# Attention of a two-layer DiT on one core: the last heads' group with its context blocks first and output-projection pieces between its steps, and the queries' rotary product moved from POOL to VectorE

## The chip, the core and the metric

The kernel runs on one core of a Trainium2 chip. A core has TensorE (matrix products; PE in the profile, its weight loads PEld), VectorE (DVE), ScalarE (ACT), GpSimd (POOL) and SyncE (SP, which here issues most of the transfers). Each engine runs its own instructions in a fixed order, written by a planner at build time from the program's dependences and order, and waits at the head of its queue. SBUF is the working memory, PSUM holds matrix products in banks of 512 columns of fp32. The metric is the device time of one execution in microseconds; comparisons go by medians of several runs.

## The reference

The model is two layers over 512 latent tokens and 256 context tokens, width 1024. Layer 0 is windowed attention (16 heads of 64, four key heads, so four heads' groups), layer 1 is retention; each layer modulates by adaLN and has a SwiGLU FFN. What the change touches is in layer 0:

```python
q_x = rope_2d(rms_norm(q_x.reshape(B, S, N_HEADS, HEAD_DIM), q_gain), tables)
...
def block(b):
    ...
    p = jax.nn.softmax(jnp.concatenate([s_ctx, s_loc, sink_col], axis=-1), axis=-1)
    return (jnp.einsum('bkgqn,bnkd->bqkgd', p[..., :L], v_c)
            + jnp.einsum('bkgqn,bnkd->bqkgd', p[..., L:L + band], vb))
o_x = jnp.moveaxis(lax.map(block, jnp.arange(nb)), 0, 1).reshape(B, S, qd)
out_x = o_x @ w_o
...
p_c = jax.nn.softmax(jnp.concatenate([s_c, sink_col], axis=-1), axis=-1)
out_c = jnp.einsum('bkgqn,bnkd->bqkgd', p_c[..., :L], v_c).reshape(B, L, qd) @ w_o
...
x = x + mx[2] * out_x
x = x + mx[5] * swiglu(modulate(rms_norm(x, norm2_g[i]), mx[3], mx[4]), ffn_w_in[i], ffn_w_out[i])
```

Latent queries of a 128-token block attend to their window and to all context keys; context queries to the context alone. The context stream runs through the same output projection and FFN.

## The kernel before

Tokens lie on the free axis and features on the partitions, in eight chunks of 128 (KT = 8). Large products are made of three fp32r matmuls (`mm3`, lines 148 to 150): each operand is split into a high and a low part, and hi·hi, lo·hi and hi·lo are added in PSUM. A weight tile of 128x1024 is loaded by SP (`w_raw`, line 122, two buffers), cast by ScalarE into its high part (line 140) and subtracted by VectorE into its low part (line 141); `w_parts` says in which pool the two halves lie (two buffers each in `rp`, which lives to the end, and some in the pool of the stage).

Attention runs in four heads' groups, g = 0 to 3. In each group come four latent blocks of 128 queries, (0, 0) to (0, 3), and two context blocks, (1, 0) and (1, 1). A block (`attend`) has three steps. `score` (line 684) makes the scores of four heads on TensorE; VectorE adds the mask and takes the minimum (685), ScalarE exponentiates and sums (line 101), VectorE takes the reciprocal (695) and POOL scales the probabilities (698). `turns` (704) transposes them on TensorE, two pairs of heads at a time, and ScalarE or VectorE copies the result out of PSUM (708). `output` (731) multiplies by the values. In groups 0 to 2 the result is kept raw and split later (`split_o`); in group 3 it is split straight into the operand of the output projection (line 741). `o_t[s][k]` is that operand, s being the stream (0 latent, 1 context) and k the chunk: group g makes k = 2g and 2g + 1.

`make_q` makes the queries of two heads at a time: 48 matmuls into two `pj` banks, the norm's sums (line 590), and for the latent stream the rotary embedding: a shuffle of the partitions (569, VectorE), a product with the cosines (570, POOL), one with the sines (571, VectorE), and the sum (572, VectorE), before the queries are split (578 to 581). Groups 0 to 2 hold two such calls each, behind blocks (0, 1) and (0, 3).

Behind the groups the residual streams are loaded (lines 809 and 810) and the attention's pools closed. The output projection follows in lines 821 to 835: weights in two sets of four, for each set the latent chunks d and then the context chunks. A chunk is 24 matmuls of 512 or 256 columns into a `pj` bank (two banks in all), a gated add into the residual (`gated_add`, 253), and a square added to the sum for the next norm (`add_square`, 207 to 210). Behind some chunks stand adaLN tiles (`ada_tile`): SP loads a 512 KB tile (268, three buffers), and VectorE reduces it against the condition row, once for each stream (271). Eight tiles give the last columns of shift and scale (parts 3 and 4) of the FFN. The condition row (`cond_rows`, 258) is loaded and passed through SiLU first. After the last chunks `fold_gain` (114), `rms` (217 and 194 to 198) and `latent_shape` (877 to 879) shape the FFN's operand, and the FFN's first products (X and Y) begin.

The planner may place an instruction ahead of its written place on its engine when it finds it ready; the written order is its priority. The memory of a closed pool is taken by later pools, tile by tile, when the earlier tile's last reader is done.

Of the kernel before, what the change touches and what calls it, by code (L numbers as in the profile page):

```python
# [14 lines left out]
P = 128  # L15
D = 1024
KT = D // P
# [8 lines left out]
RH = 4  # L26
EPS = 1e-6
UNITS = (4, 5, 8, 6)
WO_ADA = [(0, d) for d in range(7)] + [(1, 2)]
SPLIT_AT = (2, 4)  # L30
HALVES = (slice(0, 256), slice(256, 512))

# [17 lines left out]
def dit_kernel(ctx, tc, xT, cT, crow, small, consts, masks, tabs0, tabs1, jtab, adaQ, adaN, adaT, wst, out):  # L50
# [11 lines left out]
    def T(pool, cols, tag, bufs, dt=F32):  # L62
        return pool.tile([P, cols], dt, tag=tag, bufs=bufs, name=tag)
# [72 lines left out]
    def next_w(pool, own=2, raw=None):  # L136

        raw = raw or w_raw()
        hi, lo = w_parts(pool, own)
        nc.scalar.copy(hi, raw)  # L140
        nc.vector.tensor_tensor(lo, raw, hi, op=sub)  # L141
        return hi, lo
# [26 lines left out]
    def load_stream(s):  # L169
        res = []  # L170
        if s == 0:
            for k in range(KT):
                t = T(rp, 512, "res", 12)
                nc.sync.dma_start(t, xT[:, k, :])
                res.append(t)
        else:
            for k in range(0, KT, 2):
                t = T(rp, 512, "res", 12)
                nc.sync.dma_start(t.rearrange("p (a n) -> p a n", a=2), cT[:, k:k + 2, :])
                res += [t[:, 0:SC], t[:, SC:2 * SC]]  # L180
        return res
# [365 lines left out]
    def make_q(j, raw=None):  # L547
# [13 lines left out]
        def shape(s):  # L561
            n = NTOK[s]
            sq, qn = t_sq(n), t_hn(n)
            nc.scalar.activation(qn, o[s], AF.Identity, scale=qk_gain[:, 0:1])
            nc.scalar.activation(sq, o[s], AF.Square)
            sqs.append(sq)
            if s == 0:
                sw = t_y(s)
                nc.vector.stream_shuffle(sw, qn, swap16)
                nc.gpsimd.tensor_tensor(qn, qn, rope0[:, 0:512], op=mult)  # L570
                nc.vector.tensor_tensor(sw, sw, rope0[:, 512:1024], op=mult)
                nc.vector.tensor_tensor(qn, qn, sw, op=add)
            qa = T(ap, 512, "q", 9, F32R)
            if s == 0:
                qb = T(ap, 512, "q", 9, F32R)
            else:
                qa, qb = qa[:, 0:SC], qa[:, SC:2 * SC]
            nc.scalar.copy(qa[0:64, :], qn[0:64, :])
            nc.scalar.copy(qb[64:128, :], qn[64:128, :])
            nc.vector.tensor_tensor(qa[64:128, :], qn[0:64, :], qa[0:64, :], op=sub)  # L580
            nc.vector.tensor_tensor(qb[0:64, :], qn[64:128, :], qb[64:128, :], op=sub)
            q[2 * j, s] = qa
            q[2 * j + 1, s] = qb
# [56 lines left out]
        vt.append(v)  # L640
    psS.close()
    psA2 = At.enter_context(tc.tile_pool(name="psA2", bufs=1, reuse_waits="tile", space=PSUM))
    pS = lambda: T(psA2, 512, "S2", 3)

    run_dep = mybir.DependencyInfo(mybir.DependencyClass.Sync, mybir.DependencyReason.DATA)
    o_raw = {}
# [98 lines left out]
            dst = o_raw[g, s, b // 2].rearrange("p (e b q) -> p e b q", e=2, b=2)[:, :, b % 2, :]  # L745
            nc.vector.tensor_copy(dst, O.rearrange("p (e q) -> p e q", e=2))

    def attend(g, s, b):
        blk = Block(g, s, b)
        for i in range(4):  # L750
            blk.score(i)
        blk.turns()
        blk.output()

    def split_o(g):
        for e in range(2):
            hi, lo = t_h(0), t_h(0)
            for bp in range(2):
                cs = slice(bp * 256, bp * 256 + 256)
                split(o_raw[g, 0, bp][:, e * 256:e * 256 + 256], hi[:, cs], lo[:, cs])  # L760
            o_t[0][2 * g + e] = (hi, lo)
            oc = t_h(1)
            split(o_raw[g, 1, 0][:, e * 256:e * 256 + 256], oc[:, 0:SC], oc[:, SC:])
            o_t[1][2 * g + e] = (oc[:, 0:SC], oc[:, SC:])
# [30 lines left out]
    nc.vector.tensor_scalar(dcol[:, 2, :], lg[:, 4:8], 384.0, None, op0=mult)  # L795
    nc.vector.tensor_scalar(dcol[:, 3, :], lg[:, 4:8], -1.0, None, op0=mult)

    for g in range(NKV):
        for i, (s, b) in enumerate(((0, 0), (0, 1), (0, 2), (0, 3), (1, 0), (1, 1))):
            attend(g, s, b)  # L800
            if g < NKV - 1 and i in (1, 3):
                for piece in make_q(2 * g + 2 + i // 3):
                    piece()
            if (g, i) == SPLIT_AT:
                split_o(0)
                split_o(1)
        if g == 2:
            split_o(2)
    xr = load_stream(0)
    cres = load_stream(1)  # L810
    At.close()
    AK.close()
    PLAIN, ADA_FROM = 2, 4
# [2 lines left out]
    E = ExitStack()  # L816
    ep = E.enter_context(tc.tile_pool(name="ep", bufs=1, reuse_waits="tile"))
    wo_p = A.enter_context(tc.tile_pool(name="wo", bufs=1, reuse_waits="tile"))
    wsel[0] = 0
    ada_wo = [(part, d) for part in (3, 4) for d in range(4, KT)]  # L820
    for d4 in range(0, KT, 4):
        w = [next_w(wo_p) for _ in range(4)]
        if d4 == 0:
            cr = cond_rows(wo_p)
        for s, res in ((0, xr), (1, cres)):
            for d in range(d4, d4 + 4):
                o = pj(NTOK[s])
                project(w[d - d4], o_t[s], o)
                ins = gated_add(s, 0, 2, d, o, res)
                add_square(s, d, res[d])  # L830
                if (s, d) in WO_ADA:
                    ada_tile(0, *ada_wo.pop(0), (0, 1), cr, [ins], wo_p)
                if s == 1 and d == 4:
                    ln_exp_turn()
                    rms(0)
    assert not ada_wo
    A.close()

# [963 lines left out]
```

## Time and profile before

| what | value |
|---|---|
| time, median of 3 runs | 1770.04 us (1766.15 to 1770.12) |
| the profiled execution | 1767.17 us, its span 1765.4 us |
| instructions | 27623 |
| granted TensorE clock | 0.996 |
| waits of TensorE's weight queue for POOL's scaling (698), 84 to 263 us | 10.9 us in 33 |
| first and last reduction of the adaLN tiles (271) | at 322.65 and 361.38 us |
| first matmul of the FFN | at 376.97 us |
| transfers over the span | 206.68 MB, mean 117 GB/s |

A row of a group of instructions reads: source line, engine, operation, out<-in, shape, count, then busy time and mean duration in ns of one, then the idle time of the engine just before them and what ended it. A row of the timeline reads: start and duration in us, engine, line, operation, and in brackets the idle time before it with its releaser. A row of stages reads: the stretch and its length, then busy us and count for each engine, the clock, the share of the DMA engines and GB/s.

### The profile page before, as it was taken

How to read it: one execution, taken by the hardware profiler on the slowest of the kernel's cores; microseconds unless marked ns; L12 is line 12 of the kernel's file. 1: busy time of each engine (PE TensorE's matmuls, PEld its weight loads, DVE VectorE, ACT ScalarE, POOL GpSimd, SP SyncE). 2: the span in 40 equal slices, each digit the busy share in tenths (PEclk: the TensorE clock that was granted, in tenths of full speed). 3: DMA queues.
4: the chain of work that ended last, by engine and by line, in shares of the span. 5: the costliest groups of instructions: out<-in, count | busy, mean ns of one | idle time of the engine just before them, and what ended most of it. 6: DMA issues, size and time to landing. Idle time of an engine off the chain costs nothing.

```text
span 1765.4 us, 27623 instructions
## 1 busy us (share of the span) xinstructions
PE 1713.7 (97%) x10852; PEld 1526.2 (86%) x10852; DVE 1347.7 (76%) x2357; ACT 845.4 (48%) x1485; POOL 139.0 (8%) x275
## 2 busy tenths in 40 slices
PE   6899999999999999999998999999999999999999
PEld 4787776799999999999987888898897889999998
DVE  6687777788778787877799758758767897777774
ACT  5476677464434333343464534524525564445442
POOL 0034444000000000000010000000000000000000
PEclk9999999999999999999998999999999999999999
DMA  9501011533343435344343434434433223233322
GB/s 344 232 25 37 25 37 49 191 122 117 96 132 120 144 120 155 108 144 129 98 133 121 155 97 131 155 108 132 144 108 107 96 86 113 89 108 108 97 84 84
DMA packets 59890, 206.68 MB, mean 117 GB/s; under 512 B 6640, under 2 KB 7024, under 8 KB 59504
## 3 DMA queue, kind: packets, MB, share of 16 engines
q1 hardware_dynamic: 52848, 179.75, 31.4%
q0 software_dynamic: 6912, 25.17, 4.6%
q8 instruction: 85, 1.39, 0.3%
q14 instruction: 45, 0.37, 0.1%
HBM read 202.80 MB, written 2.10 MB: 116 GB/s over the span
## 4 chain that ended last, share of the span: by engine, by line
PE 76%; DVE 13%; ACT 4%; DMA 4%; issue 2%; POOL 1%; SPq 0%; ACTq 0%; DVEq 0%; POOLq 0%
PE Y L846 14%; PE Z L846 7%; PE pj L149 6%; PE pj L150 6%; PE pj L148 6%; PE Y L1191 4%; PE X L846 3%; PE Z L1204 3%; DMA wraw<-in_wst_dram 2%; DVE wlo L166 2%; PE pT L704 2%; PE pO L731 2%; PE pj L1204 2%; PE S L684 1%; PE X L1191 1%
## 5 line engine op out<-in xcount | busy, mean ns | idle before, releaser
L165 ACT CAST whi<-wraw 128x1024 fp32r<-128x1024 f32 x177 | 185.6, 1051 | 307.0 <-PE Z L150 71.5
L166 DVE TENSOR_TENSOR wlo<-wraw,whi 128x1024 fp32r<-128x1024 f32 x177 | 216.0, 1223 | 41.7 <-ACT whi L165 41.3
L846 PE MATMUL Y<-aq,whi 128*128 128x384 f32 x640 | 173.6, 335 | 0.8 <-ACT hn L984 0.8
L253 DVE SCALAR_TENSOR_TENSOR res<-pj,mod,res 128x512 f32<-128x512 f32 (+1 forms) x112 | 81.7, 730 | 71.2 <-PE pj L150 70.0
L141 DVE TENSOR_TENSOR wlo<-wraw,whi 128x1024 fp32r<-128x1024 f32 x80 | 98.1, 1227 | 34.4 <-ACT whi L140 33.6
L140 ACT CAST whi<-wraw 128x1024 fp32r<-128x1024 f32 x80 | 84.0, 1050 | 72.6 <-PE Z L150 23.2
L846 PEld LDWEIGHTS Y<-aq,whi 128*128 128x128 f32 x640 | 116.7, 188 | 2.1 <-ACT hn L984 1.6
L271 DVE CUSTOM_DVE_ANT_0 y<-adaw,crow,small_sb 128x1024 bf16<-128x1024 f32 x64 | 82.0, 1280 | 33.9 <-DMA adaw<-in_adaT_dram 33.6
L846 PE MATMUL Y<-aq,wlo 128*128 128x384 f32 x320 | 107.0, 335 | 0.0
L1204 PE MATMUL Z<-whi,sA 128*128 128x512 f32 x256 | 81.0, 392 | 0.6 <-ACT whi L165 0.6
L101 ACT ACTIVATE pr<-pr,stat,qs 128x513 f32<-128x513 f32 (+2 forms) x96 | 74.2, 777 | 12.2 <-DVE stat L691 12.0
L698 POOL TENSOR_SCALAR pr<-pr,stat 128x512 f32<-128x512 f32 (+2 forms) x96 | 67.8, 719 | 84.4 <-DVE stat L695 53.3
L148 PE MATMUL pj<-ax,whi 128*128 128x512 f32 x176 | 68.7, 391 | 1.2 <-DVE res L253 1.2
L150 PE MATMUL pj<-ax,whi 128*128 128x512 f32 x176 | 68.7, 390 | 0.0
L149 PE MATMUL pj<-ax,wlo 128*128 128x512 f32 x176 | 68.5, 389 | 0.0
L268 POOL DMA_DIRECT2D adaw<-in_adaT_dram x48 | 25.6, 533 | 517.1 <-DVE mod L271 419.8
L148 PE MATMUL pj<-act,whi 128*128 128x512 f32 x168 | 66.0, 393 | 0.0
L149 PE MATMUL pj<-act,wlo 128*128 128x512 f32 x168 | 65.9, 392 | 0.0
L150 PE MATMUL pj<-act,whi 128*128 128x512 f32 x168 | 65.5, 390 | 0.0
L704 PE MATMUL pT<-const_sb,pr 128*128 128x128 f32 x352 | 58.2, 284 | 6.7 <-POOL pr L698 3.8
L685 DVE CUSTOM_DVE_ANT_0 pr<-S,mask,qs 128x256 f32<-128x256 f32 (+1 forms) x96 | 53.0, 568 | 11.9 <-PE S L684 9.9
L704 PEld LDWEIGHTS pT<-const_sb,pr 128*128 128x128 f32 x352 | 38.7, 140 | 26.6 <-POOL pr L698 17.4
(518 smaller groups left out, 5281.4 us busy)
## 6 DMA issues: line engine op xcount, KB each, us to landing
wraw<-in_wst_dram SPq DMA_DIRECT2D x238, 512.0 KB, 3.7
adaw<-in_adaT_dram POOLq DMA_DIRECT2D x48, 512.0 KB, 3.8
wx<-in_wst_dram SPq DMA_DIRECT2D x24, 512.0 KB, 4.5
adan<-in_adaQ_dram SPq DMA_DIRECT2D x16, 512.0 KB, 8.4
adan<-in_adaN_dram SPq DMA_DIRECT2D x16, 512.0 KB, 8.7
res<-in_xT_dram SPq DMA_DIRECT2D x16, 256.0 KB, 3.9
adaw<-in_adaT_dram SPq DMA_DIRECT2D x8, 512.0 KB, 4.0
aq<-in_adaN_dram SPq DMA_DIRECT2D x12, 256.0 KB, 6.0
```

Of the source, the lines that this page charges most:

```text
L140: nc.scalar.copy(hi, raw)
L141: nc.vector.tensor_tensor(lo, raw, hi, op=sub)
L148: nc.tensor.matmul(o, whi, xhi, start=first, stop=False)
L149: nc.tensor.matmul(o, wlo, xhi, start=False, stop=False)
L150: return nc.tensor.matmul(o, whi, xlo, start=False, stop=last)
L165: nc.scalar.copy(hi, t)
L166: return nc.vector.tensor_tensor(lo, t, hi, op=sub)
L271: after(nc.vector.tensor_tensor_reduce(junk, w, cr[:, s * 1024:(s + 1) * 1024], 1.0, sm_t[:, C_ADAB + l * 48 + j:C_ADAB + l * 48 + j + 1], ...
L704: nc.tensor.transpose(tp[:, i * P:(i + 1) * P], self.pr[hd][:, ki * P:(ki + 1) * P], ident)
L846: nc.tensor.matmul(o, p, r, start=first and k + i == 0, stop=k == 3 and i == 2, skip_group_check=not first)
L1191: ins = nc.tensor.matmul(o[:, e * SC:(e + 1) * SC], p[:, ws], r, start=first and k + e + i == 0, stop=k == 3 and i == 2, skip_group_check= ...
L1204: ins = nc.tensor.matmul(o, p, r, start=first and k + i == 0, stop=k == 3 and i == 2, skip_group_check=not first)
```

## The change

The rotary's cosine product moves from POOL to VectorE. The loop over the groups ends at group 2; group 3 is written out, with its two context blocks first. Four weight sets (d = 0 to 3) are loaded and split before group 3: two in `rp`, one in the attention's pool, one (`key_room_w`) in four of the eight half-width tiles that held keys. `attend` takes pieces of work: the first stands between a block's scores and its transposes, the others between the transposes and the value product. The pieces are k = 0 to 5 of latent chunks 0 and 1, the whole context chunks 0 to 3, and behind the last block k = 0 to 5 of latent chunk 2. Context chunk 3 and latent chunk 2 use banks of the scores. After the last block come k = 6 and 7 of latent chunks 0 to 2, and then the remaining chunks: latent 3 to 7, context 4 to 7. The eight adaLN tiles now stand behind latent chunks 3 to 7 (one, two, two, two, one), where they stood behind latent chunks 0 to 6 and context chunk 2. The later weight sets (d = 4 to 7) lie in `rp`, the stage's pool twice, and `rp`.

```diff
-WO_ADA = [(0, d) for d in range(7)] + [(1, 2)]
+WO_ORDER = [(0, d) for d in range(3, KT)] + [(1, d) for d in range(4, KT)]
+WO_ADA = {(0, 3): 1, (0, 4): 2, (0, 5): 2, (0, 6): 2, (0, 7): 1}
...
-                nc.gpsimd.tensor_tensor(qn, qn, rope0[:, 0:512], op=mult)
+                nc.vector.tensor_tensor(qn, qn, rope0[:, 0:512], op=mult)
...
-    pS = lambda: T(psA2, 512, "S2", 3)
+    pS = lambda n=512: T(psA2, 512, "S2", 3)[:, :n]
...
-    def attend(g, s, b):
+    def attend(g, s, b, *fills):
         blk = Block(g, s, b)
         for i in range(4):
             blk.score(i)
+        for f in fills[:1]:
+            f()
         blk.turns()
+        for f in fills[1:]:
+            f()
         blk.output()
...
-    for g in range(NKV):
-        for i, (s, b) in enumerate(((0, 0), (0, 1), (0, 2), (0, 3), (1, 0), (1, 1))):
+    latent, context = ([(s, b) for b in range(n)] for s, n in ((0, 4), (1, 2)))
+    for g in range(NKV - 1):
+        for i, (s, b) in enumerate(latent + context):
             attend(g, s, b)
-            if g < NKV - 1 and i in (1, 3):
+            if i in (1, 3):
                 for piece in make_q(2 * g + 2 + i // 3):
                     piece()
             if (g, i) == SPLIT_AT:
                 split_o(0)
                 split_o(1)
-        if g == 2:
-            split_o(2)
+    split_o(2)
     xr = load_stream(0)
     cres = load_stream(1)
+    streams = ((0, xr), (1, cres))
+    def cut(w):
+        return [tuple(t[:, k * P:(k + 1) * P] for t in w) for k in range(KT)]
+    def key_room_w():
+        raw, hi, lo = w_raw(), [], []
+        for c in range(2):
+            hi.append(T(akv, 512, "k", 8, F32R))
+            lo.append(T(akv, 512, "k", 8, F32R))
+            split(raw[:, 512 * c:512 * c + 512], hi[c], lo[c])
+        return [(hi[k // 4][:, k % 4 * P:k % 4 * P + P], lo[k // 4][:, k % 4 * P:k % 4 * P + P]) for k in range(KT)]
+    wo = [cut(next_w(ap, 1)), cut(next_w(ap, 1)), key_room_w(), cut(next_w(ap, 1))]
+    begun = {}
+    def out_part(s, d, k0, k1, bank=pj):
+        if k0 == 0:
+            begun[s, d] = bank(NTOK[s])
+        for k in range(k0, k1):
+            mm3(begun[s, d], wo[d][k], o_t[s][k], k == 0, k == KT - 1)
+        if k1 < KT:
+            return None
+        ins = gated_add(s, 0, 2, d, begun[s, d], streams[s][1])
+        add_square(s, d, streams[s][1][d])
+        return ins
+    early = [(0, 0, 0, 3), (0, 0, 3, 6), (1, 0, 0, KT), (1, 1, 0, KT), (1, 2, 0, KT), (0, 1, 0, 6)]
+    for (s, b), part in zip(context + latent, early):
+        fills = [lambda: out_part(*part)]
+        if (s, b) == latent[-1]:
+            fills.append(lambda: out_part(1, 3, 0, KT, pS))
+        attend(NKV - 1, s, b, *fills)
+    out_part(0, 2, 0, 6, pS)
+    for d in range(3):
+        out_part(0, d, 6, KT)
     At.close()
     AK.close()
...
-    wsel[0] = 0
     ada_wo = [(part, d) for part in (3, 4) for d in range(4, KT)]
-    for d4 in range(0, KT, 4):
-        w = [next_w(wo_p) for _ in range(4)]
-        if d4 == 0:
-            cr = cond_rows(wo_p)
-        for s, res in ((0, xr), (1, cres)):
-            for d in range(d4, d4 + 4):
-                o = pj(NTOK[s])
-                project(w[d - d4], o_t[s], o)
-                ins = gated_add(s, 0, 2, d, o, res)
-                add_square(s, d, res[d])
-                if (s, d) in WO_ADA:
-                    ada_tile(0, *ada_wo.pop(0), (0, 1), cr, [ins], wo_p)
-                if s == 1 and d == 4:
-                    ln_exp_turn()
-                    rms(0)
+    for wsel[0] in (0, 2, 3, 1):
+        wo.append(cut(next_w(wo_p)))
+    cr = cond_rows(wo_p)
+    for s, d in WO_ORDER:
+        ins = out_part(s, d, 0, KT)
+        for _ in range(WO_ADA.get((s, d), 0)):
+            ada_tile(0, *ada_wo.pop(0), (0, 1), cr, [ins], wo_p)
+        if (s, d) == (1, 4):
+            ln_exp_turn()
+            rms(0)
```

## The prediction

> **What bounds the kernel now.** I read the page first (busy shares, then the chain that ended last), then the busy time of each engine by stage, then the matrix groups of the stages that the change touches, then the waits and the timeline around them.
>
> ```profile
> PE 1713.7 (97%) x10852; PEld 1526.2 (86%) x10852; DVE 1347.7 (76%) x2357; ACT 845.4 (48%) x1485; POOL 139.0 (8%) x275
> ...
> PE 76%; DVE 13%; ACT 4%; DMA 4%; issue 2%; POOL 1%; SPq 0%; ACTq 0%; DVEq 0%; POOLq 0%
> ```
>
> TensorE is the bound: 97% busy, 76% of the chain. A gain must therefore come out of time in which TensorE has nothing to do. The next fence shows four stretches: heads' group 1, group 2, the last group (3) and the rest of the output projection (columns: stretch, length, then busy us of PE, PEld, DVE, ACT, POOL, clock, DMA).
>
> ```profile
> 150.20:206.45 56.25, 53.76 (x380) 42.71 (x378) 39.32 (x130) 37.54 (x86) 25.58 (x50) 1.00 0.07 20
> 206.45:262.20 55.75, 54.36 (x385) 43.28 (x385) 43.40 (x140) 42.40 (x102) 24.78 (x50) 1.00 0.12 39
> 262.20:320.30 58.10, 54.04 (x359) 38.74 (x357) 41.32 (x154) 41.74 (x109) 23.74 (x56) 1.00 0.21 72
> 320.30:376.80 56.50, 56.10 (x336) 49.78 (x337) 44.80 (x75) 20.62 (x29) 0.00 (x0) 1.00 0.41 132
> ```
>
> The clock is full in all four, so lost time is waiting. The busy column leaves 4.06 us free in the last group (58.10 - 54.04), but ends of matmuls are modelled and overlap, so I count the work instead: instructions by their start-to-start steps.
>
> ```profile
> L704 PE MATMUL pT<-const_sb,pr 128*128 128x128 f32 x104 | 18.3, 286 | 1.9 <-POOL pr L698 1.5
> L684 PE MATMUL S<-kc,q 128*128 128x256 f32 x63 | 13.6, 303 | 0.0
> L731 PE MATMUL pO<-tt,v 128*64 128x256 f32 x106 | 13.4, 387 | 0.1
> L148 PE MATMUL pj<-h,whi 128*128 128x512 f32 x18 | 7.6, 421 | 2.0 <-ACT whi L140 2.0
> L150 PE MATMUL pj<-h,whi 128*128 128x512 f32 x16 | 6.6, 410 | 0.0
> L149 PE MATMUL pj<-h,wlo 128*128 128x512 f32 x16 | 6.5, 405 | 0.0
> L684 PE MATMUL S<-k,q 128*128 128x384 f32 x16 | 4.4, 358 | 0.0
> L684 PE MATMUL S<-k,q 128*128 128x256 f32 x16 | 3.8, 307 | 0.0
> ```
>
> The steps, from the timeline of TensorE (start, us, instruction):
>
> ```profile
> 326.09 0.39 PE L150 MATMUL pj<-h,whi 128*128 128x512 f32 x1
> ...
> 330.85 0.39 PE L150 MATMUL pj<-h,whi 128*128 128x512 f32 x1
> 331.08 0.28 PE L148 MATMUL pj<-hc,whi 128*128 128x256 f32 x1
> ...
> 332.14 0.28 PE L148 MATMUL pj<-hc,whi 128*128 128x256 f32 x1
> ...
> 123.05 1.09 PE L704 MATMUL pT<-const_sb,pr 128*128 128x128 f32 x8
> ...
> 308.58 1.95 PE L731 MATMUL pO<-tt,v 128*64 128x256 f32 x16
> ```
>
> 512 columns: 21 steps in 4.76 us, 0.227 each. 256 columns: 9 steps in 1.06, 0.118. 384 columns: 0.17, in proportion. Transposes and value products: (1.09 - 0.27)/7 = 0.117 and (1.95 - 0.38)/15 = 0.105; I take 0.11 for both. The last group then holds 210 x 0.11 + 79 x 0.118 + 16 x 0.17 + 50 x 0.227 + 0.4 (four norm products) = 46.9 us of work in 58.1: **11.2 us empty**. Of that work 11.4 us are 50 matmuls of the output projection that already stand between the attention steps (latent chunks d=0 and d=1; two PSUM banks hold no more).
>
> Group 1, where two query projections fill, by the same count:
>
> ```profile
> L704 PE MATMUL pT<-const_sb,pr 128*128 128x128 f32 x88 | 14.4, 285 | 2.4 <-POOL pr L698 1.2 <-DVE tt L708 1.0
> L731 PE MATMUL pO<-tt,v 128*64 128x256 f32 x88 | 10.8, 386 | 0.1
> ...
> L590 PE MATMUL pj<-const_sb,sq 128*128 128x2 f32 x27 | 3.3, 235 | 0.0
> ```
>
> With its 64 + 16 scores and 48 + 48 query matmuls (read from the loops) that is 176 x 0.11 + 64 x 0.118 + 16 x 0.17 + 48 x 0.345 + 27 x 0.11 = 49.2 us, so 7.0 us empty in 56.25; group 2 likewise about 6. What empties TensorE there is seen in the list of who waits for POOL's scaling:
>
> ```profile
>   PEld pT L704: 17.4, 52
>   PE pT L704: 3.8, 10
> ```
>
> Over the four groups, transposes stand 21.2 us, in 62 waits, behind L698: 5.3 us a group. TensorE runs in a fixed order and holds a transpose at the head while later matmuls could run.
>
> [...]
>
> **The change part by part.** *Last group: context first, and pieces between the steps.* The context's blocks come before the latent ones, so that context chunks of the output projection become possible inside the group. Work between the steps grows from 11.4 us to four context chunks (4 x 24 x 0.118 = 11.3) and k=0..5 of three latent ones (3 x 18 x 0.227 = 12.3): 23.6 us. The same matmuls leave the stretch behind; the sum is unchanged, and only emptiness counts. The end of the group shows one stall that goes:
>
> ```profile
> 319.18 0.49 PE L148 MATMUL pj<-h,whi 128*128 128x512 f32 x1 [1.40 <-ACT whi L140]
> ...
> 320.29 0.50 PE L148 MATMUL pj<-h,whi 128*128 128x512 f32 x1 [0.62 <-ACT whi L140]
> ```
>
> There the weights of d=2 and d=3 are split only when the attention's room is free. After the change all four sets are split before. Bounds for what stays empty: at worst the 11.2 of now (gain 0); at best 3 us, some half of a filled group (gain 8.2). A filled group keeps 6 to 7; but now a chunk of 2 to 4 us is written between scores and transposes of each block, longer than the waits for L698 (21.2/62 = 0.34 each), so about a third of those goes too. I take 4.5 us: **gain 6.7**.
>
> At nothing I cost: the splits made earlier (two weight sets more in the group, some 2.1 us of ScalarE and 2.4 of VectorE, and two half-width instructions more for the set kept in the keys' room), since ScalarE and VectorE are busy 41.7 and 41.3 of 58.1; without that cover, some 2 us. The loads behind them: SP issued d=2's and d=3's raw weights before the group's middle already, and the stream reloads keep their place. Four context gated adds (0.48) with their squares move into the group, into the same cover. Two PSUM banks of the scores are lent out only from the last block on.
>
> *Behind attention: the adaLN tiles.* Eight tiles, each of two reductions, stood behind eight chunks; now they stand behind five.
>
> ```profile
> 313.85 0.33 SPq L258 DMA_DIRECT2D crow<-in_crow_dram  x1
> ...
> 322.65 1.28 DVE L271 CUSTOM_DVE_ANT_0 junk<-adaw,crow,small_sb 128x1024 bf16<-128x1024 f32 x1 [0.93 <-ACT crow L107]
> ...
> 358.91 0.75 DVE L253 SCALAR_TENSOR_TENSOR res<-pj,mod,res 128x512 f32<-128x512 f32 x1 [1.68 <-PE pj L150]
> ...
> 361.38 1.28 DVE L271 CUSTOM_DVE_ANT_0 junk<-adaw,crow,small_sb 128x1024 bf16<-128x1024 f32 x1
> ...
> 373.54 0.75 DVE L877 SCALAR_TENSOR_TENSOR act<-res,acol,y 128x512 f32<-128x512 f32 x1
> ...
> 376.97 0.34 PE L148 MATMUL X<-aq,whi 128*128 128x384 f32 x1
> ```
>
> Let T be the end of the last value products. TensorE then needs 18 x 0.227 + 120 x 0.227 + 96 x 0.118 + 0.5 (the sum for the norm) = 43.1 us to the FFN. The condition row's room lies, as I add up the pools, under d=1's weights, which are read until T+3.5; from its issue to the first reduction it took 8.8 us (322.65 - 313.85), so reductions start at T+12.3. VectorE then serves tile 1 to T+14.9; behind d=4 (TensorE done T+15.0) 0.75 + 0.69 + 4 x 1.28 to T+21.7; d=5 to T+28.2, and a weight split 1.22; d=6 to T+36; d=7 with one tile to T+40. The FFN's shaping (L877) needs the last tile's column. It now starts 3.4 us ahead of the FFN's first matmul (376.97 - 373.54) and would start some 3 ahead, but with VectorE busy up to there and the second FFN weight's buffer free only after the last context chunk. I take **1.5 us lost**; bounds 0, and 6 where the gated adds queue behind all reductions (d=7's at T+36 instead of T+32, and 1.5 us more in the shaping).
>
> *Queries' rotary wholly on VectorE.* Eight products of 128x512 leave POOL:
>
> ```profile
> L570 POOL TENSOR_TENSOR hn<-hn,rope x8: 1279/1746/1785, 85.0 to 254.1; 128x512 f32<-128x512 f32 x8
> ...
> L571 DVE TENSOR_TENSOR y<-y,rope x8: 683/947/1790, 85.4 to 254.1; 128x512 f32<-128x512 f32 x8
> ...
> 99.31 0.69 DVE L571 TENSOR_TENSOR y<-y,rope 128x512 f32<-128x512 f32 x1
> ...
> 101.17 0.69 DVE L572 TENSOR_TENSOR hn<-hn,y 128x512 f32<-128x512 f32 x1 [1.17 <-POOL hn L570]
> ```
>
> VectorE stands 1.17 us at the head of its queue while POOL finishes. In place of that stand 0.69 us of its own product: 1.17 - 0.69 = 0.5 saved. The chain of waits goes through this step at 99, 198 and 253 us, and at 85 us the two products stretched each other (1.79 against 0.69). I take 4 x 0.5: **gain 2.1**. Bounds: all eight, 4.6 gained; all eight products added in full where VectorE sets the path, 8 x 0.69 = 5.5 lost.
>
> Sum against the profiled execution's span: 1765.4 - 6.7 + 1.5 - 2.1 = 1758.1. That execution took 1767.17 with 1.8 outside the span, 2.9 under the median of 1770.04; the same 7.3 off the median is **1762.7**.
>
> **The rivals.** (A) *The pieces do not fill.* The second projection bank goes to latent d=1 from the start, as now, and holds it until the last block; context chunks wait for the end. For it: in the group now both banks are held so. Against it: the text takes it for the context first. Then 11.2 us stay, 1.5 are lost behind, 2.1 gained: about 1769.5.
>
> (B) *The adaLN tiles set the end.* If they keep the pace of now, 40.0 us from the first to the last (322.65 to 362.66), the last ends at T+52.3, the shaping follows in 2 us, and the FFN starts at T+54.6, 11.5 late instead of 1.5. 1770.04 - 6.7 + 11.5 - 2.1 = **1772.7**, slower. It decides from T+41 on. For it: three buffers, loads behind weight loads on one queue. Against it: the pace of now is mostly that of the chunks (5.4 us each).
>
> (C) *VectorE's new products hurt POOL's scaling.* L698 is 0.69 undisturbed for 512 columns and up to 1.84; eight times some 0.6 longer, with transposes waiting, is 4.8 lost in place of 2.1 gained: 1769.6. [...]
>
> (D) *More goes than I take.* 3 us stay empty, nothing is lost behind, all eight rotaries pay: 1770.04 - 8.2 - 4.6 = 1757.2.
>
> **How the numbers follow.** Forecast 0.50 (own range 1757 to 1768), A 0.18, B 0.14, C 0.08, D 0.10. What can be told from no change is 0.3%, 5.3 us: below 1764.7 or above 1775.3. Faster: 0.39 of the forecast's 0.50, D, and a little of A: 0.51. Slower: B's upper part, where strict order adds to the pace, and mixtures of B and C: 0.14. Same: 0.35. The range reaches to D's lower side and past B: 1754 to 1774.
>
> **What would show it.** Right: the last group and what follows up to the FFN's first X product 5 to 8 us shorter; four context chunks (matmuls on hc) ahead of the last value products; L140's wait at the group's end gone; L570's rows on DVE near 0.69 with L572 right behind. Wrong: no hc projection matmuls before the last block (A); VectorE with reductions up to the FFN's start and a wait of X for aq (B); L698's median above 0.75 (C); or time that comes or goes outside 84 to 400 us, for which I have no term.

## The result, and the profile after

The changed kernel takes 1774.28 us (median of 11 executions, 1772.73 to 1776.01) against 1770.12 for the kernel before on the same chip: ratio 1.0027, 95% interval 1.0017 to 1.0036. One execution of the kernel before took 2584.7 us and stands outside the ratio. The changed kernel is slower, by 4.8 us with an interval of 3.0 to 6.4 (what the ratio exceeds 1 by, times 1770), where 1762.7 was forecast; that is less than the 0.3% that the prediction called no change, but the interval does not contain a ratio of 1. The time lies 0.3 us above the range. The profiled execution has a span of 1772.5 us.

The head of the page after, to be read beside the first fence of the prediction:

```profile
PE 1716.1 (97%) x10852; PEld 1528.1 (86%) x10852; DVE 1351.8 (76%) x2366; ACT 845.4 (48%) x1486; POOL 125.9 (7%) x267
...
PE 75%; DVE 14%; DMA 4%; ACT 3%; issue 2%; POOL 2%; SPq 0%; DVEq 0%; ACTq 0%; POOLq 0%
```

The same matmuls; 13 us of POOL went and only 4 us of VectorE came in their place. Nothing here tells where the time went. For that I set marks that both kernels pass with the same TensorE work between the first and the last: the first score, the first value products of group 2, those of group 2's last block, those of the last block of all, the FFN's first X product (the prediction has it for before, 376.97), and the norm products behind the FFN's first part. TensorE's timeline has them, first before, then after (start, us, instruction):

```profile
101.70 0.68 PE L684 MATMUL S<-k,q 128*128 128x256 f32 x1
...
225.28 0.44 PE L731 MATMUL pO<-tt,v 128*64 128x256 f32 x2
...
276.43 0.44 PE L731 MATMUL pO<-tt,v 128*64 128x256 f32 x2
...
316.70 0.44 PE L731 MATMUL pO<-tt,v 128*64 128x256 f32 x2
...
415.43 0.33 PE L315 MATMUL pj<-const_sb,sq 128*128 128x128 f32 x1
```

```profile
103.81 0.36 PE L685 MATMUL S<-k,q 128*128 128x256 f32 x1
...
228.36 0.44 PE L732 MATMUL pO<-tt,v 128*64 128x256 f32 x2
...
280.46 0.44 PE L732 MATMUL pO<-tt,v 128*64 128x256 f32 x2
...
328.80 0.44 PE L732 MATMUL pO<-tt,v 128*64 128x256 f32 x2
...
379.56 0.41 PE L149 MATMUL X<-aq,whi 128*128 128x384 f32 x1
...
422.71 0.33 PE L316 MATMUL pj<-const_sb,sq 128*128 128x128 f32 x1
```

The differences, for these two and for the kernels of the experiments (a: groups 0 and 1 from the first score on; b: group 2; c: the last group; d: behind the attention to X; e: the FFN's first part; last, the ratio to before over all executions with its interval):

| kernel | a | b | c | d | e | sum | ratio |
|---|---|---|---|---|---|---|---|
| before | 123.6 | 51.2 | 40.3 | 60.3 | 38.5 | 313.7 | |
| before, second profile | 123.6 | 51.2 | 40.3 | 61.9 | 38.5 | 315.5 | |
| changed | 124.5 | 52.1 | 48.3 | 50.8 | 43.1 | 318.9 | 1.0027 (1.0017 to 1.0036) |
| e1 rotary back on POOL | 123.6 | 52.8 | 48.9 | 50.8 | 43.1 | 319.2 | 1.0020 (1.0011 to 1.0029) |
| e2 rotary alone | 124.7 | 50.8 | 40.8 | 61.3 | 38.4 | 316.0 | 1.0028 (1.0018 to 1.0038) |
| e3 changed, no adaLN tiles | 124.7 | 52.1 | 48.3 | 50.1 | 40.7 | 315.8 | 1.0010 (1.0001 to 1.0018) |
| e6 e1, no pieces | 123.5 | 52.7 | 43.0 | 62.3 | 42.7 | 324.2 | 1.0048 (1.0034 to 1.0061) |
| e13 context first alone | 123.7 | 50.7 | 42.3 | 63.2 | 38.6 | 318.4 | 1.0017 (1.0008 to 1.0026) |

From the first score to the norm products the change loses 5.2 us: 0.9 in a, 0.9 in b, 8.0 - 9.5 = -1.5 in c and d together, and 4.6 in e. What lies behind e (1349.9 and 1349.8 us) is the same. The profiled span grew by 7.1: the rest, 2.1, stands ahead of the first score (101.7 and 103.8 us), where the second profile of the same kernel before reads 103.2, so a single profile can't assign it. Against the 8.0 us that the last group grew, 9.5 come back behind it, so the pieces did move; c and d together gained 1.5, where the prediction's two terms for them came to 5.2 (6.7 - 1.5). Stretches of the table with a fall of TensorE's clock read longer for it: d of the second profile by 1.6, c of e13 by up to 1.8, c of e6 by up to 3.6 and its e by up to 1.7 (the lengths of the falls are given below, and for e in e6 the clock was 0.53 from 390.6 to 394.2).

### The profile page after: what moved, and what is told of

Same layout as the page of the kernel before. It is cut to its first block, busy times and chain, and to the rows that moved or that the text cites. A ratio compares the mean times of both kernels' runs of the same rounds, so it can differ in the third digit from the quotient of the medians.

```text
span 1772.5 us, 27621 instructions
## 1 busy us (share of the span) xinstructions
PE 1716.1 (97%) x10852; PEld 1528.1 (86%) x10852; DVE 1351.8 (76%) x2366; ACT 845.4 (48%) x1486; POOL 125.9 (7%) x267
## 4 chain that ended last, share of the span: by engine, by line
PE 75%; DVE 14%; DMA 4%; ACT 3%; issue 2%; POOL 2%; SPq 0%; DVEq 0%; ACTq 0%; POOLq 0%
PE Y L883 14%; PE Z L883 7%; PE pj L149 6%; PE pj L151 6%; PE pj L150 6%; PE X L883 3%; PE Z L1241 3%; PE Y L1228 3%; DMA wraw<-in_wst_dram 3%; DVE wlo L167 3%; PE pT L705 2%; PE pO L732 2%; PE pj L1241 1%; PE X L1228 1%; POOL pr L699 1%
## 5 line engine op out<-in xcount | busy, mean ns | idle before, releaser
L167 DVE TENSOR_TENSOR wlo<-wraw,whi 128x1024 fp32r<-128x1024 f32 x177 | 216.0, 1223 | 42.3 <-ACT whi L166 41.9
```

Of the source, the lines that this page charges most:

```text
L167: return nc.vector.tensor_tensor(lo, t, hi, op=sub)
```

## The experiments

**Rotary.** e1 undoes this part in the changed kernel:

```diff
-                nc.vector.tensor_tensor(qn, qn, rope0[:, 0:512], op=mult)
+                nc.gpsimd.tensor_tensor(qn, qn, rope0[:, 0:512], op=mult)
```

> The changed kernel with the cosine product of the queries' rotary back on POOL, all else kept. Theory R (the rotary on VectorE is what makes the attention late: by the last group's start the changed kernel is 4.1 us behind): the time goes 3 to 4 us down from the changed kernel's 1774.3, to about 1770.5, and the last context block's first value products of group 2 come near 276.4 instead of 280.5. The prediction's own term (the move gains 2.1): 1776.4. If the lateness comes from another part of the change: 1774, unchanged.

It gave 1774.54 us, ratio 1.0020 (1.0011 to 1.0029) against the change's 1.0027. The difference, 1.2 us with an interval of some -1.1 to 3.6, is not clear of noise, so what the rotary costs in the whole change stays open within it; the sums of marks, 319.2 and 318.9, show no loss. Stretch a is back at 123.6, but b and c are longer than in the change, which I had not expected. e2 makes the opposite edit in the kernel before and nothing else:

> The kernel before with the cosine product on VectorE, and nothing else of the change. Theory R: 3 to 4 us slower than before, about 1773.5. The prediction's term: 2.1 faster, 1768. If the order of the last group is what moved the queries: no change, 1770.

1776.39 us, ratio 1.0028 (1.0018 to 1.0038): alone, the rotary costs about 5 us (3.2 to 6.7), of which 2.3 show in the sum of marks of its profiled execution, the fastest of its seven (1773.53). Stretch a is about 1.0 us longer in each of the kernels with the rotary on VectorE (changed, e2, e3). The move does at its own place what was forecast. VectorE in the changed kernel (start, us, instruction):

```profile
99.80 0.75 DVE L570 STREAM_SHUFFLE y<-hn 128x512 f32<-128x512 f32 x1
100.58 0.69 DVE L571 TENSOR_TENSOR hn<-hn,rope 128x512 f32<-128x512 f32 x1
101.19 0.68 DVE L572 TENSOR_TENSOR y<-y,rope 128x512 f32<-128x512 f32 x1
101.91 0.69 DVE L573 TENSOR_TENSOR hn<-hn,y 128x512 f32<-128x512 f32 x1
```

From shuffle to sum 2.11 us against 2.63 before (98.54 to 101.17): the 0.5 is there. It is not there four times, though. Who waited for POOL's product in the kernel before (total us, times):

```profile
  DVE hn L572: 2.9, 3
```

Two of these waits are 1.17 us long and one is 0.58, so no more than about 1.0 us could be saved at the stalls themselves. The rest of the effect is elsewhere. Who waited for POOL's scaling (total us, times), in e2 and then in the changed kernel; the prediction quotes 17.4 and 3.8 for before:

```profile
  PEld pT L704: 24.3, 52
  PE pT L704: 9.1, 14
```

```profile
  PEld pT L705: 21.0, 48
  PE pT L705: 7.8, 16
```

21.2 us of waits became 33.4 in e2; in stretch a alone they rose from 11.9 to 18.9, where TensorE passes the marks only 1.1 us later. So the transposes wait longer for the scaling, and most of these waits are not lost time. Why the scaling comes later is not shown. One reading is that the product that left POOL now stands on VectorE ahead of the softmax statistics; but POOL's idle time before L698 that ended with one of the two statistics was 83.1 us before (53.3 with the reciprocal, 29.8 with the other) and 85.3 in e2 (69.8 and 15.5), hardly more.

**Order and pieces.** e6 takes the pieces out of e1's last group; e13 is the kernel before with only the order changed:

```diff
-        fills = [lambda: out_part(*part)]
...
-        attend(NKV - 1, s, b, *fills)
...
-    out_part(0, 2, 0, 6, pS)
-    for d in range(3):
-        out_part(0, d, 6, KT)
+        attend(NKV - 1, s, b)
+    for s, n in ((0, 3), (1, 4)):
+        for d in range(n):
+            out_part(s, d, 0, KT)
```

> The kernel of e1 with every matmul of the output projection behind the last group; the context blocks still come first. From the value products of group 2's last block to the FFN's first X product before takes 100.6 us and e1 99.7. The prediction's step (pieces fill time in which TensorE is empty): some 8 us of the 19.5 us of pieces lose their cover, X comes 5 to 8 us later than in e1, the time is 1780 to 1782. Theory E (a piece between the steps lengthens the group by about its own length, the emptiness stays at 6 to 7 us): X comes within 2 us of e1, the time is 1773 to 1776.

```diff
-        for i, (s, b) in enumerate(((0, 0), (0, 1), (0, 2), (0, 3), (1, 0), (1, 1))):
+        blocks = [(0, 0), (0, 1), (0, 2), (0, 3), (1, 0), (1, 1)]
+        if g == NKV - 1:
+            blocks = blocks[4:] + blocks[:4]
+        for i, (s, b) in enumerate(blocks):
```

> The kernel before with the last group's two context blocks ahead of its latent blocks, and nothing else of the change. Theory C (four context blocks in a row starve TensorE): from group 2's first value products to the last group's last ones the way is 1.5 to 2 us longer than before (91.5), and the end of the attention, now a latent block of five key tiles, shows its stall for the split weights as before: 1771.5 to 1772. Rival (the pieces cost it): within 0.5 us of before, 1769 to 1770.

e6: 1779.54 us, 5.0 more than e1 (by the ratios; some 2 to 8), so the pieces do fill something. e13: 1773.42 us, ratio 1.0017 (1.0008 to 1.0026): the order alone costs 3.0 us (1.4 to 4.6). The busy time of the engines from the value products of group 2's last block to the last ones, in before, e13, e6 and the changed kernel (stretch, length, PE, PEld, DVE, ACT, POOL, clock, DMA):

```profile
276.30:317.40 41.10, 40.08 (x274) 28.45 (x274) 26.96 (x100) 28.23 (x74) 18.01 (x40) 1.00 0.15 46
```

```profile
276.20:320.20 44.00, 39.23 (x267) 27.54 (x265) 26.28 (x93) 28.26 (x72) 19.17 (x40) 0.96 0.23 83
```

```profile
278.70:323.40 44.70, 40.45 (x266) 28.27 (x265) 25.83 (x97) 28.42 (x72) 18.03 (x40) 0.92 0.17 60
```

```profile
280.40:330.40 50.00, 48.61 (x358) 38.59 (x357) 30.33 (x109) 30.57 (x79) 18.06 (x40) 1.00 0.07 23
```

PE reads 89 to 98% busy throughout. By the prediction's count of matmuls at their steps the four hold 34.7, 32.5, 32.0 and 43.6 us of work: 6.4, 11.5, 12.7 and 6.4 us are empty. (The prediction's 11.2 was counted from 262.20 to 320.30, with 14 us of group 2 ahead of this stretch and the two stalls behind it.) (In e13 and e6 the clock was lower for some 4 and 8 us, the 0.96 and 0.92 of the rows, which takes up to 1.8 and 3.6 us off their emptiness.) So the group in the new order is emptier than in the old one by some 3 to 5 us (e13: 5.1, or 3.3 without the clock's share), and draws only 3.9 us of the projection into itself (e13) where before it was 6.8; the 14.2 us that run in it in the changed kernel bring the emptiness back to where it was. The 1.5 that c and d gained are about the two stalls at the group's end (1.40 and 0.62 us), which went: by the same count TensorE was empty for 3.7 us between the last value products and X before, and for 1.9 after. Not all pieces came to run there: the 18 matmuls of d=2 that are written ahead of the end stand behind the last value products.

```profile
330.36 0.39 PE L732 MATMUL pO<-tt,v 128*64 128x256 f32 x2
330.68 0.50 PE L149 MATMUL S<-h,k 128*128 128x512 f32 x1
```

e14 keeps e1's pieces and puts group 2's context blocks between its latent blocks, so that never four short context blocks stand in a row:

```diff
-        for i, (s, b) in enumerate(latent + context):
+        for i, (s, b) in enumerate(latent[:2] + context + latent[2:] if g == NKV - 2 else latent + context):
```

> The kernel of e1 with group 2's context blocks between its latent blocks (0,1) and (0,2), so that no more than two context blocks stand in a row. Theory C: the way from group 2's first value products to the last ones of the last group falls from 101.7 to 100 us, the time from 1774.5 to 1773. Rival: unchanged, or longer because the four latent blocks are broken up, 1774.5 to 1776.

1776.03 us, ratio 1.0033 (1.0021 to 1.0046): b grew to 55.8 and c fell by 0.7 only. Theory C, that it is the four in a row, is not borne out; that the order opens the emptiness is shown by e13, why is not.

**The 1.6 us in group 2** (52.8 in e1) were put down to early splits of d=2's weights, which stand there on VectorE. e5 and e9:

```diff
-    wo = [cut(next_w(ap, 1)), cut(next_w(ap, 1)), key_room_w(), cut(next_w(ap, 1))]
+    wo = [cut(next_w(ap, 1)), cut(next_w(ap, 1))]
...
+        if (s, b) == latent[0]:
+            wo += [key_room_w(), cut(next_w(ap, 1))]
```

> The kernel of e1 (1774.5) with the weights of d=2 and d=3 split behind the last group's two context blocks instead of ahead of the group. In e1 the stretch from group 2's first value products to its last block's is 52.8 us long against 51.2 before, and d=2's half-width split instructions stand in it at 226 to 229, ahead of a softmax statistic. Theory S (these instructions are the 1.6): the stretch is 51.2 again and the time 1.5 us lower, 1773. Rival (the stretch is longer for another reason, or the split costs as much in the last group): 1774.5.

```diff
-                    split(O[:, e * P:e * P + P], hi[:, cs], lo[:, cs])
+                    out_split.append(split(O[:, e * P:e * P + P], hi[:, cs], lo[:, cs]))
...
-            split(raw[:, 512 * c:512 * c + 512], hi[c], lo[c])
+            after(split(raw[:, 512 * c:512 * c + 512], hi[c], lo[c]), [out_split[0]])
...
-    wo = [cut(next_w(ap, 1)), cut(next_w(ap, 1)), key_room_w(), cut(next_w(ap, 1))]
+    wo = [cut(next_w(ap, 1)), cut(next_w(ap, 1))]
...
+        if (s, b) == context[1]:
+            wo += [key_room_w(), cut(next_w(ap, 1))]
```

> The kernel of e1 with an ordering that really holds d=2's two half-width splits behind the last group's first context block (in the kernel of e5 they kept their place in group 2, so that run told nothing of them). Theory S: the stretch from group 2's first value products to its last block's falls from 52.7 to 51.2, and of the 1.5 us at least half stays to the FFN's first X: 1773 to 1774. Rival (the splits cost as much in the last group, where the keys' room is wanted at once): group 2 at 51.2, the last group 1.5 longer, 1774.5.

e5 left the instructions where they were; the first row below is e5's, the second e9's (count, then min, median and max ns, then first and last start):

```profile
L167 DVE TENSOR_TENSOR k<-wraw,k x2: 686/950/1215, 226.4 to 228.2; 128x512 fp32r<-128x512 f32 x2
```

```profile
L167 DVE TENSOR_TENSOR k<-wraw,k x2: 682/686/690, 289.0 to 290.3; 128x512 fp32r<-128x512 f32 x2
```

A line moved in the text does not move its instruction when the planner sets the order: 1774.6 us, 1.0025 (1.0015 to 1.0035). With VectorE's two instructions really moved (one of ScalarE's two casts stayed, at 224.1), b became longer, 53.9, and the time 1776.59, 1.0046 (1.0033 to 1.0058). Theory S has fallen for VectorE's part. e13, without early weights, has 50.7 in b and e6, with them and without pieces, 52.7: the lengthening goes with the weight sets and stream loads brought forward, but which of their instructions does it stays open.

**Behind the attention.** e3 leaves the eight adaLN tiles out:

```diff
-            ada_tile(0, *ada_wo.pop(0), (0, 1), cr, [ins], wo_p)
+            part, dd = ada_wo.pop(0)
+            for c in range(2):
+                nc.vector.memset(mods[0, c][:, part, dd:dd + 1], 0.0)
```

> The changed kernel without the eight adaLN tiles behind the attention (their loads, their sixteen reductions and the condition row are left out, the columns are set to zero). Theory T (VectorE, full with reductions from 348 to 375, makes the FFN's shaping late): the FFN's first X product comes some 2 us earlier against the last value products and the stalls of TensorE between 380 and 400 go, together 4.5 to 6 us: about 1769. Rival (the second FFN weight, split only at 380 to 383, is what is late): 1773 to 1774, with X waiting for its weights.

1772.39 us, ratio 1.0010 (1.0001 to 1.0018): by the ratios 3.0 us less than the changed kernel (some 0.7 to 5.3); 3.1 by the marks (0.7 in d, 2.4 in e). VectorE and TensorE in the last 30 us ahead of the FFN and the first 14 of it, changed kernel, before, e3:

```profile
346.00:376.00 30.00, 29.18 (x157) 24.63 (x157) 29.84 (x48) 9.35 (x13) 0.00 (x0) 1.00 0.48 157
376.00:390.00 14.00, 10.81 (x61) 7.99 (x61) 14.00 (x27) 11.63 (x21) 0.00 (x0) 1.00 0.34 112
```

```profile
343.00:373.00 30.00, 29.60 (x160) 25.18 (x159) 21.72 (x36) 8.58 (x13) 0.00 (x0) 1.00 0.26 83
373.00:387.00 14.00, 14.00 (x91) 13.29 (x90) 13.90 (x24) 12.13 (x23) 0.00 (x0) 1.00 0.40 118
```

```profile
346.00:376.00 30.00, 29.60 (x168) 25.53 (x167) 13.26 (x22) 7.86 (x13) 0.00 (x0) 1.00 0.15 47
376.00:390.00 14.00, 12.11 (x70) 10.47 (x70) 12.80 (x23) 12.80 (x23) 0.00 (x0) 1.00 0.45 144
```

The third busy time of a row is VectorE's: 29.84 + 14.00 = 43.84 of 44 us in the changed kernel, 35.62 before, 26.06 in e3. It still shapes the FFN's operands when TensorE already multiplies them:

```profile
384.26 0.44 PE L149 MATMUL X<-aq,whi 128*128 128x384 f32 x1 [0.69 <-ACT aq L915]
385.44 0.44 PE L151 MATMUL X<-aq,whi 128*128 128x384 f32 x1 [0.57 <-DVE aq L916]
386.63 0.45 PE L151 MATMUL X<-aq,whi 128*128 128x384 f32 x1 [0.41 <-DVE aq L916]
388.35 0.44 PE L151 MATMUL X<-aq,whi 128*128 128x384 f32 x1 [0.39 <-DVE aq L916]
```

In the kernel before the profile shows no wait of TensorE's matmuls in this stretch. The tiles are not all of it: without them e is 40.7, still 2.2 longer than before. There VectorE has some room (12.80 of 14 us), and TensorE waits for operands from ScalarE and once for the second weight's low part:

```profile
383.70 0.44 PE L149 MATMUL X<-aq,whi 128*128 128x384 f32 x1 [0.96 <-ACT aq L916]
384.76 0.45 PE L150 MATMUL Y<-aq,wlo 128*128 128x384 f32 x1 [0.45 <-DVE wlo L142]
```

What makes these 2.2 us stays open. They are not the pieces' alone: e is long in e6 too, which has none (42.7, at most 1.7 of it the clock's), and not in e13 (38.6).

e4 and e8 start the tiles earlier: e4 by the room of the condition row, e8 (on e1) by that of three tiles too, placed behind the gated adds of d=0 to 2:

```diff
+    cr = cond_rows(wo_p)
     for wsel[0] in (0, 2, 3, 1):
         wo.append(cut(next_w(wo_p)))
-    cr = cond_rows(wo_p)
```

> The changed kernel with the condition row loaded ahead of the last four weights, in the first room of the pool instead of the fifth. If the row's lateness (issued 7.5 us behind the last value products) sets when VectorE's reductions end: with a room that comes free 4 to 7 us earlier the reductions end by that much earlier and the time falls 3 to 5 us, to about 1770. If the shaping is late for the weights' split or the last chunks: 1774. If the room frees no earlier: 1774 and the row is issued near 338 still.

```diff
-WO_ADA = {(0, 3): 1, (0, 4): 2, (0, 5): 2, (0, 6): 2, (0, 7): 1}
+WO_ADA = {(0, 3): 1, (0, 4): 1, (0, 5): 1, (0, 6): 1, (0, 7): 1}
...
-    for d in range(3):
-        out_part(0, d, 6, KT)
+    done = [out_part(0, d, 6, KT) for d in range(3)]
...
+    cr = cond_rows(wo_p)
+    for ins in done:
+        ada_tile(0, *ada_wo.pop(0), (0, 1), cr, [ins], wo_p)
     for wsel[0] in (0, 2, 3, 1):
         wo.append(cut(next_w(wo_p)))
-    cr = cond_rows(wo_p)
```

> The kernel of e1 with the condition row and the first three adaLN tiles in the first rooms of the pool, ahead of the weights, and these three tiles behind the gated adds of d=0 to 2 instead of d=4 to 6. Theory T (the reductions end too late because they start too late): they start within 12 us of the last value products instead of 17.8, end some 6 us earlier, the FFN's start (43.1) comes near the 40.7 of the kernel without tiles, and the time falls by 2.5 to 3.5 us to 1771.5. Rival (the rooms come free no earlier, or the loads stand behind weights): the reductions start at 17 again, 1774.5.

e4 was 1777.62 us, 1.0034 (1.0022 to 1.0046): the row was issued at 325.3 instead of 337.9, yet the first reduction stayed 17.9 us behind the last value products: the tiles' own loads stood behind two weight loads on SP's queue and were issued 11.2 us behind them, as in the changed kernel. e8, 1774.43 us, 1.0023 (1.0014 to 1.0032), e 41.8: the reductions started 15.0 us behind them and 1.3 us came back in e, but d lost 1.0: TensorE stood 1.19 us at 355.07 for a gated add on VectorE. e7 and e10 gave the weights other rooms, so that the FFN's second one is free earlier:

```diff
-    for wsel[0] in (0, 2, 3, 1):
+    for wsel[0] in (0, 1, 2, 3):
```

> The kernel of e1 with the rooms of the last four weights in the order 0, 1, 2, 3 instead of 0, 2, 3, 1, so that the room which the FFN's second weight takes is read last by d=5 and not by d=7. Theory W (the two weight splits that stand on VectorE at 8.7 and 10.3 us behind the FFN's first X are late for this room and stretch the FFN's start): the stretch from the first X to the next norm products falls from 43.1 to 41 us, the time to 1772.5. Theory T alone (the reductions' tail is all of it): 43.1 still, 1774.5.

```diff
-    for wsel[0] in (0, 2, 3, 1):
+    for wsel[0] in (0, 2, 1, 3):
         wo.append(cut(next_w(wo_p)))
+    wsel[0] = 3
```

> The kernel of e1 with the last four weights in the rooms 0, 2, 1, 3 and the FFN's first three weights in the order shared, shared, own, so that its second one waits for d=6's last product instead of d=7's. Theory W (the second and third split at 8.7 and 10.3 us behind the first X stretch the FFN's start): one split moves ahead of X + 2, the stretch from X to the norm products falls from 43.1 to 41 us, the time to 1772.5. Rival (all of the 4.7 us is VectorE's backlog of reductions and shaping, in whatever order): 43 us still, 1774.5.

1777.43 us, 1.0041 (1.0028 to 1.0054), and 1776.48, 1.0045 (1.0032 to 1.0057); e was 43.7 in both, 0.6 longer than in e1; e7 lost 1.6 in d as well, and most of what e10 lost by its ratio lies outside the marks and is not explained. In e10 the second weight was cast at 375.91, ahead of X at 378.43, and yet its split came at 387.85:

```profile
375.91 1.06 ACT L141 CAST whi<-wraw 128x1024 fp32r<-128x1024 f32 x1 [0.45 <-PE pj L151]
```

```profile
387.85 1.22 DVE L142 TENSOR_TENSOR wlo<-wraw,whi 128x1024 fp32r<-128x1024 f32 x1
```

In the 11.94 us between, VectorE was busy for 11.75: with the tiles there it is not the room that is late, but VectorE's queue. Theory W has fallen for the kernel with its tiles. e12 has the edits of e9 and e10 together:

> The kernel of e1 with both edits of e9 and e10. If S and W both hold and add: group 2 at 51.2, the FFN's start at 41, 1771, the same as before within what can be told. If neither: 1774.5.

1776.51 us, 1.0045 (1.0031 to 1.0059), as either alone. e15 takes other work off VectorE there:

```diff
-        add_square(s, d, streams[s][1][d])
+        add_square(s, d, streams[s][1][d], eng=nc.gpsimd if d > 3 else nc.vector)
```

> The kernel of e1 with the sums of squares of the output projection's chunks d=4 to 7 (four of 0.69 and four of 0.42 us on VectorE, 4.4 us in all) on POOL, which is empty behind the attention. Theory T (VectorE's backlog from 346 to 390 us sets the FFN's start): the reductions end some 2.5 us earlier, the stretch from the FFN's first X to the norm products falls from 43.1 to 40 to 41 us, the time to 1772. Rival (X waits for something else): 43 us and 1774.5; slower if POOL's slower sums make the norm of the latents late.

1777.85 us, 1.0051 (1.0037 to 1.0065). e fell to 41.7, but d rose by 5.3. The greater part is one wait of TensorE, for the last latent sum on POOL, with which the norm begins; the expectation had named it as a possibility:

```profile
372.83 2.07 PE L218 MATMUL pj<-y,ones_sb 128*128 128x512 f32 x2 [4.26 <-POOL y L211]
```

The sum took POOL about 1.5 us where VectorE took 0.69, and the gated add ahead of it came late on VectorE, at 369.70 (364.91 in e1). Around this stall the clock was 0.51 from 370.6 to 377.6. Besides, POOL's sums stretch VectorE's reductions, which they were to relieve. POOL and VectorE side by side, and VectorE's sixteen reductions as a group (busy, mean ns):

```profile
364.56 1.47 POOL L211 TENSOR_TENSOR y<-y,sq 128x512 f32<-128x512 f32 x1 [5.28 <-ACT sq L210]
```

```profile
364.93 2.19 DVE L272 CUSTOM_DVE_ANT_0 junk<-adaw,crow,small_sb 128x1024 bf16<-128x1024 f32 x1
...
L272 DVE CUSTOM_DVE_ANT_0 junk<-adaw,crow,small_sb 128x1024 bf16<-128x1024 f32 x16 | 23.8, 1488 | 0.3
```

The reduction at 364.93 takes 2.19 us in place of 1.28. Four of the sixteen are stretched, each while a sum runs on POOL (2.19, 2.18, 2.19 and 1.89); the sixteen take 23.8 in place of 20.5. The one at 364.93 ran beside POOL's sum for 1.10 us, up to 366.03 (364.56 + 1.47), and ended at 367.12; no run shows what makes these reductions longer. e16 has the edits of e8, e14 and e15:

> The kernel of e8 (condition row and first tiles in the first rooms) with the edits of e14 and e15 as well. If C and T both hold and add to the 1.4 us that e8's FFN start gained: 1769.5 to 1771, the same as before. If neither: 1774.5.

1780.89 us, 1.0058 (1.0046 to 1.0071): what e14 and e15 lose stays lost. No version beat the kernel before.

**The kernel before once more**, for the scatter of a single profile:

> The kernel before once more, for a second profile: its first profiled execution (1767.2) is 3 us under its median. If the stages up to 430 us repeat within 0.3 us and the difference lies in the later stages, the shares of the change's 4 us can be read from the marks of single profiles up to there. Otherwise they can be read to 1 us only.

Ratio 1.0000 (0.9990 to 1.0010), span 1770.4 against 1765.4. Of the 5.0 between the spans, 1.5 stand ahead of the first score and 1.8 behind the norm products. Between these marks only d differs, by 1.6 us, and the clock column says why:

```profile
323.00:326.60 3.60, 3.60 (x10) 2.82 (x9) 1.68 (x3) 3.50 (x4) 0.00 (x0) 0.53 0.87 272
```

Eight 512-column steps took 0.43 us each in place of 0.227. The other stretches repeat to 0.1 us.

## Why the prediction was wrong, step by step

1. **"A filled group keeps 6 to 7; but now a chunk of 2 to 4 us ... I take 4.5 us: gain 6.7"** is the step that failed most. It took the emptiness of the old order as the stock that the pieces would fill, and the new order as free. The order alone cost 3.0 us (e13); it opened some 3 to 5 us of emptiness in the last group, and the pieces filled about that. Empty were 6.4 us after and 6.4 before, between the same marks. c and d together gained 1.5, about the stalls of L140 that went. Of the 23.6 us of pieces 4.1 (d=2) did not run inside. Why the new order is emptier stays open (e14).
2. **"The condition row's room lies ... under d=1's weights, which are read until T+3.5"** was mis-sized because d=2's piece did not run inside: its eighteen matmuls stood between, so d=1's weights were read until T+7 and the row was issued at T+7.5 (T is here the start of the last value product, 330.4). With the tiles' own loads behind weights, the reductions started at T+17.9 instead of T+12.3 and ended at T+44.8 instead of T+40.
3. **"I take 1.5 us lost; bounds 0, and 6"**: up to X, where the sum ended, this was near: X came at T+49.2 behind 47.2 us of work, 2.0 lost. What failed is that the sum ended there. The FFN's first part, e, had no term, and it grew by 4.6. VectorE was busy up to the FFN and past it, as rival B had it; leaving the tiles out gave back 3.0 (e3), 2.4 of them in e, and the other 2.2 of e stay open. The second weight's buffer, the other reason that was given, made no difference when it came free earlier (e10). B's price of 11.5 was not reached because the reductions ran back to back, 26.8 us from first to last, not at the pace of 40.
4. **"I take 4 x 0.5: gain 2.1"** had the wrong sign for the move alone, which cost about 5 us (e2), at the bound of "5.5 lost" that was named. The 0.5 at the stall is there, but a stall of that length stood twice, not four times, and transposes wait 12 us more for the scaling in e2; what delays the scaling is not shown. In the whole change the move's part, 1.2 (1.0027 against 1.0020), is not clear of noise.
5. **"At nothing I cost: the splits made earlier"**: b grew by 1.6 in e1. The early weight sets go with it (e6 against e13); VectorE's two half-width instructions are not the cause (e9).
6. Right: four context chunks ran ahead of the last value products; L140's stall at the group's end went; the rotary rows on VectorE were 0.69 us with the next right behind; TensorE's work behind the attention came to 47.2 us by the count, 43.1 without d=2's 4.1, as summed. Rival A is out (the pieces ran), C too as it was put (the scaling's median was 0.696 us, no longer than before; in e2, where its median is 0.698, transposes wait longer for it all the same).

Put together, by the ratios: the order +3.0 (1.4 to 4.6) by its own run; pieces, early weights and bunched tiles +0.5 from there to e1 (1.0020 against 1.0017); the rotary +1.2 from there to the change. The last two steps are each within the noise. By the marks the second is no small effect but two that cancel: from e13 to e1 up to 3.7 us are saved to X, and 4.6 given back in the FFN's first part.

## What to carry to other kernels

Emptiness of the bounding engine is a property of one order of the work: after a reordering, count it anew before pricing what may fill it. A stall that an instruction ends is not its price: count how often it stands at that length, and measure the move by itself. Work that an engine did under cover of a long stretch is not covered any more when the stretch is shortened: sum that engine's work against the new length, and on to the next stage.

## What the runs showed of the hardware

TensorE's granted clock fell in some stretches to 0.51 to 0.53, for 3.6 or 7.0 us at a time (0.53 from 311.0 to 314.6 in e13, 0.51 from 312.0 to 319.0 in e6), in one execution of a kernel and not in another: at 323.0 in the second profile of before, not in the first, though both had the same stalls of TensorE just before (1.4 and 0.6 us). The fall at 323.0 (0.53 over 3.6 us) cost 1.6 us, a third of the whole effect studied here. The falls in e13 and e15 stand near stalls of TensorE (1.07, 0.34 and 0.79 us within 5 us before e13's, 4.26 at e15's), but the stalls ahead of 323.0 stand in the first profile of before too, without a fall. No run here shows what sets a fall off.
